# Masked attention: the first 512 columns of each unit but a job's last are turned by DMA and multiplied one unit later

## The chip, the cores and the metric

The kernel runs on one core of one Trainium2 chip. The metric is the device time of one execution in microseconds (us). The engines are named as in the profile: PE (TensorE, matmuls; PEld are its weight loads), DVE (VectorE), ACT (ScalarE), POOL (GpSimd) and SP (SyncE, which issues the DMA transfers here). Each engine executes its own instructions in order and waits on semaphores for the others.

## The reference, cut to what matters

Two layers over 1024 tokens of width 1024. Layer one holds a sparse attention ("A", in which a top-256 selection masks the keys) and a banded attention ("B"); layer two holds three kinds of one attention ("C") and a latent attention ("D"). The change touches A only:

```python
def dsa_attention(q, k, v, qi, ki, wi, k_sel):
    ...
        score = jnp.where(causal[None], score, -jnp.inf)
        _, idx = lax.top_k(score, k_sel)
        ...
        s = jnp.einsum('bqgrd,bqkgd->bqgrk', qb, ks) * scale
        p = masked_softmax(s, valid[:, :, None, None, :])
        o = jnp.einsum('bqgrk,bqkgd->bqgrd', p.astype(v.dtype), vs)
```

There are 8 blocks of 128 queries, and 8 heads that share keys and values in two groups of four. The kernel computes all causal scores and adds a mask of the selection, which gives the same softmax.

## The kernel before, in words

*Jobs and units.* `attn_gen` (L618) writes all four attentions as a list of jobs. A job of A (`job_a`, L1007) is one block i of 128 queries and one group g of four heads; its row of keys has nk = 128 (i + 1) columns. The list of A is g = 0, i = 0 to 7, then g = 1, i = 0 to 7 (L1183). A job is cut into units of `per` heads, four where nk is up to 256, two up to 512, one above. So i = 0, 1 have one unit, i = 2, 3 two, i = 4 to 7 four.

*One unit.* PE multiplies queries and keys into PSUM (L680, tile psS, up to 512 columns at a time). DVE adds the mask, takes the row extreme and writes the row to SBUF (L683, tile pt, three buffers). ACT prepares the bias (L687) and takes exp in place (L689). The values are then multiplied with the weights p, and for that p must lie with keys on the partitions: it has to be turned, and it is needed as a 16-bit high part and a 16-bit low part. A unit's columns are turned in groups of up to four tiles of 128 x 128, and each group goes one way:

- `p`: four PE transposes into PSUM (L730, psT), ACT copies the high part (L733, hp), DVE subtracts for the low part (L734);
- `q`: the same transposes, ACT copies the PSUM tile to SBUF (L737, sg), POOL makes the high part (L738) and the low part (L739). sg has the tag of hl, so both share its two buffers (HLB = 2);
- `d`, `g`, `l`: no PE transpose. ACT copies the high part straight from pt (L710, hl), DVE (`d`) or POOL (`g`, `l`) subtracts for the low part (L711), and one DMA transpose on SP's queue turns both into ht (L713, two buffers, HTB = 2).

After that PE multiplies three times per tile (L660, L661, L663). With `l` the multiplication is put on the list `late` (L715) and written behind the last group of the following unit (L744).

*Which way.* L705 gives `l` to the first group of a unit if the job says `late` and the unit isn't the job's last; otherwise the way is the next one of a cycle (`WAYS`): 'ppq' for A with g = 0, 'pq' with g = 1. Jobs of C (two of its three kinds) and D already say `late`, and their cycles hold 'p' alone. B has the cycle 'g'.

*Order.* Turning is written some groups behind the scores (`tlag`, L801), the values behind that. `L.run` (L1183) puts other work, the fill, beside attention at a ratio of the costs that the yields name: projections that are still missing, loading the output-projection weights, and `mix_ab` (rows of the finished attention are loaded, gated and turned by POOL and PE, and split by ACT and DVE). The output projection itself (`c_out`, L520 to L522, added to x at L1160) is written after the attention. This written order is a priority only: a planner orders each engine's instructions ahead of the run by its own cost estimates, takes an instruction when its inputs and a buffer are there, and so also moves later work, such as the output projection, into gaps. The reloads of x (L1201) use large buffers that masks, keys and other tiles hold until A's scores are done.

Of the kernel before, what the change touches and what calls it, by code (L numbers as in the profile page):

```python
# [184 lines left out]
def trunk(ctx: ExitStack, tc: tile.TileContext, A, out):  # L185
# [430 lines left out]
    ways = [cycle(w) for w in WAYS]  # L616
# [152 lines left out]
    def softmax_norm(mul=None):  # L769

        def norm(nm, sm, box, sink=None):
            yield
            if sink is not None:
                es = st.tile([P, 4], F32, name="es")
                V.tensor_tensor(es, nm, sink, OP.subtract)
                yield
                S.activation(es, es, AF.Exp)
                yield
                V.scalar_tensor_tensor(sm, sm, 1e-30, es, op0=OP.max, op1=OP.add)
            else:  # L780
                V.tensor_scalar(sm, sm, 1e-30, None, op0=OP.max)
            rs = st.tile([P, 4], F32, name="rs", bufs=6)
            V.reciprocal(rs, sm)
            if mul:
                mul(rs)
            box.append(rs)
        return norm

    def causal(nk):
        return lambda c, w: mk[:, 768 - w:] if c + w == nk else mk[:, P:P + w]  # L790

    def plain(m):
        return lambda c, w: m[:, c:c + w]

    def gqa(qs, j, kst, t0):
        def passes(h):
            q = qs[:, h % 2, j, h // 2]
            return [(q, lambda a, b: kst[:, 0, t0 + a:t0 + b]), (q, lambda a, b: kst[:, 1, t0 + a:t0 + b])]
        return passes
# [4 lines left out]
    def store_o(dst, i, c0, inv):  # L804
        def fin(po, f):
            m = wk.tile([P, 256], F32, name="mx", bufs=3)
            V.scalar_tensor_tensor(m.rearrange("p (h d) -> p h d", h=4), po, inv, bcast(f, 64), op0=OP.mult,
                                   op1=OP.mult)
            if dst is not None:
                nc.sync.dma_start(dst[i * P:(i + 1) * P, c0:c0 + 256], m)  # L810
            return m
        return fin
# [12 lines left out]
    def blk(t, i):  # L825

        return t[0] if i == 2 else t[1][:, OFF[i]:OFF[i] + (i + 1) * P]
# [179 lines left out]
    def job_a(i, g):  # L1007
        def start():
            nk = (i + 1) * P
            vh, vl = B["vha"], B["vla"]  # L1010
            f0 = store_o(od if g == 0 else None, i, 256 * g, B["vsca"][0][1])

            def fin(po, f):
                B["m", i] = f0(po, f)
                L.done.add(("oa", g, i))
            mask = causal(nk) if i < 2 else plain(blk(B["hi"], i).bitcast(BF16))
            return (gqa(B["qs", "a", g, i - i % 2], i % 2, B["ka"][g], 0), mask,
                    lambda kt, h: vh[:, kt, 64 * g:64 * g + 64], lambda kt, h: vl[:, kt, 64 * g:64 * g + 64],
                    lambda h: 3e38, fin)
        need = [("qa", g, i - i % 2), ("ka", i - i % 2), ("va", i)] + ([("mask", i)] if i >= 2 else [])  # L1020
        return dict(need=need, nk=(i + 1) * P, npass=2, start=start,
                    norm=softmax_norm(), tlag=tlag, way=ways[2 + g],
                    free=give_qs if i % 2 else None)

    XS = [slot("xs", F32)[:, 0:2048].rearrange("p (j n) -> p j n", j=2) for _ in range(NT // 2)]
# [155 lines left out]
    FM = fa_then()  # L1181
    L.run(attn_gen(jobs(job_b, 0, BO[0]) + jobs(job_b, 1, BO[1])), FA, BR, aux=tk, arate=TA)
    L.run(attn_gen(jobs(job_a, 0, AO[0]) + jobs(job_a, 1, AO[1])), FM, AR, aux=tk, arate=TA)  # L1183
    L.pump(FM)
    L.flush()
# [682 lines left out]
```

## Time and profile before

| | |
|---|---|
| median of 3 executions | 1532.42 us (1530.67 to 1533.38) |
| profiled execution | 1533.38 us |
| its span | 1531.6 us |
| PE busy in the span | 1334.1 us (87%) |
| PEld busy | 1218.5 us (80%) |
| DVE busy | 1106.3 us (72%) |
| ACT busy | 940.1 us (61%) |
| POOL busy | 820.4 us (54%) |

Busy time is the time in which an engine was executing an instruction; matmuls are pipelined, so overlapping matmuls count once and a busy PE need not be at its peak. In the timeline views a row begins with the start in us and the time taken in us; "xN" is a number of merged instructions, and a bracket at the end is the idle time before it with what ended it. In the views of one tile or line, three numbers with slashes are the shortest, median and longest duration in ns.

### The profile page before, as it was taken

The page shows a single profiled execution, that of the slowest core. Times are in us where ns is not written, and L with a number is a line of the kernel's source. Part 1 is how long each engine was busy: PE and PEld are TensorE (multiplying, and loading weights), DVE is VectorE, ACT ScalarE, POOL GpSimd, SP SyncE. Part 2 cuts the span into 40 slices and gives each one's busy share as a digit, 9 for nine tenths or more (in the row PEclk, how much of TensorE's full clock was granted, in tenths as well). Part 3 has the DMA queues.
Part 4 walks back from the last instruction along what each step waited for, and adds up shares of the span by engine and source line. Part 5 has one row for each costly group of instructions (what it writes and reads, how often), then busy time and mean ns, then how long its engine had stood idle before and what let it go on. Part 6 is the DMA issues. An engine that isn't in the chain of part 4 may idle for free. (4 is left out here: it accounts for less than half of the span.)

```text
span 1531.6 us, 34278 instructions
## 1 busy us (share of the span) xinstructions
PE 1334.1 (87%) x12132; PEld 1218.5 (80%) x12132; DVE 1106.3 (72%) x3409; ACT 940.1 (61%) x2683; POOL 820.4 (54%) x1058
## 2 busy tenths in 40 slices
PE   5998889888268899999999998999988668879998
PEld 5998788878157698999999986899967456768887
DVE  5387877888977865176367677876778989987652
ACT  5355578877668864164335667846677567856531
POOL 6899549897457584235355333352233465745440
PEclk9999999999569999999999999999998869999999
DMA  6311363322132333142212434212243323334442
GB/s 202 94 29 32 73 129 81 80 55 67 26 92 61 99 109 105 43 159 66 57 28 68 100 70 84 63 51 67 60 67 73 90 63 75 68 87 104 124 129 76
DMA packets 208939, 122.83 MB, mean 80 GB/s; under 512 B 141696, under 2 KB 193664, under 8 KB 208768
## 3 DMA queue, kind: packets, MB, share of 16 engines
q1 hardware_dynamic: 208768, 120.65, 31.5%
q8 instruction: 95, 1.56, 0.4%
q14 instruction: 76, 0.62, 0.1%
HBM read 67.65 MB, written 23.07 MB: 59 GB/s over the span
## 5 line engine op out<-in xcount | busy, mean ns | idle before, releaser
L520 PE MATMUL pp<-whi,Rh 128*128 128x256 f32 (+4 forms) x1648 | 481.1, 292 | 20.8 <-DVE zst L611 8.0
L522 PE MATMUL pp<-whi,Rl 128*128 128x256 f32 (+4 forms) x1648 | 476.9, 290 | 0.0
L521 PE MATMUL pp<-wlo,Rh 128*128 128x256 f32 (+4 forms) x1648 | 475.3, 289 | 0.7 <-POOL wlo L477 0.7
L520 PEld LDWEIGHTS pp<-whi,Rh 128*128 128x128 f32 x1648 | 317.2, 193 | 27.0 <-DVE zst L611 8.1
L521 PEld LDWEIGHTS pp<-wlo,Rh 128*128 128x128 f32 x1648 | 317.1, 192 | 2.3 <-POOL wlo L477 0.9
L522 PEld LDWEIGHTS pp<-whi,Rl 128*128 128x128 f32 x1648 | 316.9, 192 | 1.1
L689 ACT ACTIVATE pt<-pt,nm 128x256 f32<-128x256 f32 (+8 forms) x384 | 244.1, 638 | 5.4
L477 POOL TENSOR_TENSOR wlo<-wraw,whi 128x256 fp32r<-128x256 f32 (+4 forms) x208 | 162.7, 792 | 137.3 <-ACT whi L476 131.4
L711 POOL TENSOR_TENSOR hl<-pt,hl 128x512 f16<-128x512 f32 x114 | 137.1, 1205 | 148.5 <-ACT hl L710 121.5
L476 ACT ACTIVATE whi<-wraw 128x256 fp32r<-128x256 f32 (+4 forms) x208 | 83.2, 416 | 128.0 <-DMA wraw<-in_cd_w_in 42.1
L730 PE MATMUL psT<-identf,pt 128*128 128x128 f32 x800 | 145.1, 286 | 11.0 <-ACT pt L689 5.1
L733 ACT ACTIVATE hp<-psT 128x512 f16<-128x512 f32 (+3 forms) x241 | 108.2, 461 | 62.4 <-PE psT L730 57.5
L734 DVE TENSOR_TENSOR hp<-psT,hp 128x512 f16<-128x512 f32 (+3 forms) x241 | 123.3, 520 | 18.2 <-ACT hp L733 16.7
L683 DVE CUSTOM_DVE_ANT_0 pt<-psS,mk 128x512 f32<-128x512 f32 (+4 forms) x208 | 107.1, 521 | 40.5 <-PE psS L680 29.3
L730 PEld LDWEIGHTS psT<-identf,pt 128*128 128x128 f32 x800 | 95.3, 145 | 23.6 <-ACT pt L689 11.4
L687 ACT ACTIVATE nm<-nm 128x1 f32<-128x1 f32 (+2 forms) x208 | 41.6, 200 | 96.4 <-DVE nm L683 95.6
L663 PEld LDWEIGHTS <-hp 128*128 128x128 f16 x800 | 72.9, 99 | 29.2 <-DVE hp L734 17.6
L660 PEld LDWEIGHTS <-hp 128*128 128x128 f16 x800 | 74.4, 99 | 22.0 <-issue 7.5
L710 ACT ACTIVATE hl<-pt 128x512 f16<-128x512 f32 x114 | 70.9, 626 | 13.9 <-DMA ht<-hl 13.3
L661 PEld LDWEIGHTS <-hp 128*128 128x128 f16 x800 | 74.6, 99 | 2.8 <-issue 1.7
L689 ACT ACTIVATION_READ_ACCUMULATOR pt<-pt,nm 128x1 f32 x384 | 73.0, 190 | 0.0
L680 PE MATMUL psS<-kd,qhl 128*128 128x512 f32 (+4 forms) x192 | 57.4, 380 | 14.5 <-DVE nm L683 11.9
(326 smaller groups left out, 3764.0 us busy)
## 6 DMA issues: line engine op xcount, KB each, us to landing
wraw<-in_cd_w_in SPq DMA_DIRECT2D x72, 128.0 KB, 2.1
wraw<-in_ab_w_in SPq DMA_DIRECT2D x56, 128.0 KB, 2.5
xs<-in_x SPq DMA_DIRECT2D x8, 512.0 KB, 6.0
od<-mx SPq DMA_DIRECT2D x32, 128.0 KB, 1.9
wraw<-in_ab_w_out SPq DMA_DIRECT2D x32, 128.0 KB, 2.2
x<-in_x SPq DMA_DIRECT2D x8, 512.0 KB, 4.5
mo<-od SPq DMA_DIRECT2D x16, 256.0 KB, 2.9
nz<-zdr SPq DMA_DIRECT2D x16, 256.0 KB, 2.9
```

The costliest lines, as they stand in the source:

```text
L476: S.activation(hi[:, :o], raw[:, :o], AF.Copy)
L477: G.tensor_tensor(lo[:, :o], raw[:, :o], hi[:, :o].bitcast(F32), OP.subtract)
L520: T.matmul(ps, xh, hi[:, :n], start=q == 0 and k == 0, stop=False)
L521: T.matmul(ps, xh, lo[:, :n], start=False, stop=False)
L522: T.matmul(ps, xl, hi[:, :n], start=False, stop=q == 3 and k == 1)
L661: T.matmul(dst, ph[:, a], vl(kt, h), start=False, stop=False)
L683: V.tensor_tensor_reduce(pt[:, j * nk + c:j * nk + c + w], ps[:, at:at + w], mask(c, w), -1.0, first, op0=OP.add, op1=OP.min, accum_out=low)
L689: S.activation(pt[:, j * nk:(j + 1) * nk], pt[:, j * nk:(j + 1) * nk], AF.Exp, scale=-1.0, bias=nm[:, h:h + 1], accum_out=sm[:, h:h + 1])
L711: (V if way[-1] == "d" else G).tensor_tensor(hl[:, w:], pt[:, o:o + w], hl[:, :w], OP.subtract)
L730: T.transpose(pT[:, a], pt[:, o:o + P], identf)
L733: S.activation(ph, pT[:, :n], AF.Copy)
L734: V.tensor_tensor(pl, pT[:, :n], ph, OP.subtract)
```

## The change

A's jobs, too, say `late=True`. L705 then gives `l` to the first group (four tiles, 512 columns) of every unit of A but a job's last; the other groups go on drawing from their cycles.

```diff
@@ job_a
         return dict(need=need, nk=(i + 1) * P, npass=2, start=start,
-                    norm=softmax_norm(), tlag=tlag, way=ways[2 + g],
+                    norm=softmax_norm(), tlag=tlag, late=True, way=ways[2 + g],
                     free=give_qs if i % 2 else None)
```

## Rows read from the trace of the kernel before

**Rows 1.** Windows: stretch, length, busy PE, PEld, DVE, ACT, POOL (count), clock, DMA share, GB/s.
```profile
447.00:525.00 78.00, 69.88 (x815) 58.58 (x813) 64.81 (x191) 67.13 (x182) 45.66 (x59) 0.98 0.23 69
525.00:600.00 75.00, 67.95 (x821) 63.10 (x819) 46.94 (x134) 49.06 (x120) 56.26 (x69) 1.00 0.41 119
600.00:700.00 100.00, 99.07 (x820) 98.05 (x821) 48.12 (x134) 34.31 (x82) 28.43 (x40) 0.98 0.25 83
```

**Rows 2.** Timeline of DVE: the instruction that closes a job.
```profile
504.81 0.47 DVE L807 SCALAR_TENSOR_TENSOR mx<-po,vs_e,rs 128x256 f32<-128x256 f32 x1
...
516.46 0.48 DVE L807 SCALAR_TENSOR_TENSOR mx<-po,vs_e,rs 128x256 f32<-128x256 f32 x1
...
601.67 0.48 DVE L807 SCALAR_TENSOR_TENSOR mx<-po,vs_e,rs 128x256 f32<-128x256 f32 x1
```

**Rows 3.** Timeline of SP's queue, then of PE, at the second half's end.
```profile
587.84 1.97 SPq L1201 DMA_DIRECT2D x<-in_x  x4
...
600.57 0.58 PE L520 MATMUL pp<-whi,Rh 128*128 128x256 f32 x1 [1.98 <-DVE x L1160]
```

**Rows 4.** Timeline of PE around one group of transposes.
```profile
556.75 0.60 PE L730 MATMUL psT<-identf,pt 128*128 128x128 f32 x4
557.11 0.36 PE L522 MATMUL pp<-whi,Rl 128*128 128x256 f32 x1
557.31 0.28 PE L520 MATMUL pp<-whi,Rh 128*128 128x256 f32 x1
557.43 0.28 PE L521 MATMUL pp<-wlo,Rh 128*128 128x256 f32 x1
```

**Rows 5.** Tiles hp and sg, 447 to 600: the ways p and q.
```profile
L733 ACT ACTIVATE hp<-psT x51: 256/576/637, 447.3 to 595.1; 128x512 f16<-128x512 f32 x27, 128x256 f16<-128x256 f32 x10, 128x128 f16<-128x128 f32 x7, 128x384 f16<-128x384 f32 x7
...
L737 ACT ACTIVATE sg<-psT x35: 278/597/633, 454.2 to 593.9; 128x512 f32<-128x512 f32 x31, 128x256 f32<-128x256 f32 x2, 128x128 f32<-128x128 f32 x1, 128x384 f32<-128x384 f32 x1
L738 POOL TENSOR_SCALAR hp<-sg x35: 323/618/644, 454.9 to 594.6; 128x512 f16<-128x512 f32 x31, 128x256 f16<-128x256 f32 x2, 128x128 f16<-128x128 f32 x1, 128x384 f16<-128x384 f32 x1
L739 POOL TENSOR_TENSOR hp<-sg,hp x35: 426/1163/1174, 455.8 to 596.6; 128x512 f16<-128x512 f32 x31, 128x256 f16<-128x256 f32 x2, 128x128 f16<-128x128 f32 x1, 128x384 f16<-128x384 f32 x1
```

**Rows 6.** Tiles hl and ht, 850 to 1220 (attention C); last, who waited for ht: us, times.
```profile
L710 ACT ACTIVATE hl<-pt x56: 614/626/668, 854.7 to 1191.7; 128x512 f16<-128x512 f32 x56
L711 POOL TENSOR_TENSOR hl<-pt,hl x56: 1152/1164/1279, 855.4 to 1192.4; 128x512 f16<-128x512 f32 x56
L713 SPq DMA_TRANSPOSE ht<-hl x56: 1231/1232/2197, 856.6 to 1194.8; - x56
...
  PE po L660: 8.5, 10
  ACT hl L710: 5.9, 10
...
DMA to landing us min/median/max: 3.0/3.1/4.8
```

**Rows 7.** Waits of ACT (total, times, longest): 447 to 525, then 525 to 600.
```profile
ACT hp L733 <- PE psT L730: 2.4, 5, 0.8
...
ACT sg L737 <- PE psT L730: 1.1, 2, 0.7
...
ACT hp L733 <- PE psT L730: 7.9, 6, 2.7
```

**Rows 8.** Windows, columns as in rows 1.
```profile
460.00:480.00 20.00, 15.93 (x191) 12.77 (x189) 13.64 (x42) 17.05 (x46) 19.59 (x28) 1.00 0.30 90
```

**Rows 9.** Waits of PE and of POOL, 525 to 600.
```profile
PE po L660 <- POOL hp L738: 2.7, 1, 2.7
PE po L663 <- POOL hp L739: 1.4, 1, 1.4
...
POOL mo L1112 <- DMA mo<-od: 1.7, 2, 1.3
```

**Rows 10.** Windows for line 520 alone: stretch, length, busy PE, PEld, clock, DMA share, GB/s.
```profile
470.00:498.00 28.00, 0.00 (x0) 0.00 (x0) 0.94 0.14 41
```

## The prediction

> **What bounds the kernel now.** I first read busy time by stretch over the whole span, to find the masked attention and what follows it. It runs from 447 to about 600 us as two halves, one per group of heads, and the table splits them [rows 1]. In the first half ScalarE (ACT) is busy 67.1 of 78 us, TensorE (PE) 69.9, VectorE (DVE) 64.8: three engines in step, none with much room. In the second half ACT falls to 49.1 of 75 while PE stays at 68.0; from 600 to 700 PE is busy 99.1 of 100. The second half is longer because output-projection matmuls, which need finished rows of both groups, come in between: PE carries both.
>
> Then the ends of jobs, by the VectorE instruction that closes each [rows 2]: the last job of the first half takes 516.46 - 504.81 = 11.65 us, 2.9 per unit (one head of 1024 keys); the second half closes 601.67 - 516.46 = 85.2 us after the first.
>
> What hands the end on is a load. The last four reloads of x go out at 587.84, when the last scores have released their buffers, and PE waits 1.98 us for them before the out-projection goes on at 600.57 [rows 3]. From there PE is full, so if the last scores come earlier by d, the kernel ends earlier by about d.
>
> **The change part by part.** Jobs i = 2, 3 have two units and i = 4 to 7 have four; all but a job's last give their first 512 columns to the new way: 2 + 12 = 14 groups per half, 28 in all, of four 128x128 tiles each. Groups no longer drawn from the cycles 'ppq' and 'pq' shift all later draws. Walking the cycles through the 86 groups gives: p 51 becomes 35, q 35 becomes 23. Of these, p of four tiles 27 to 21, q of four tiles 31 to 9, q of fewer 4 to 14.
>
> *Removed from PE.* 112 transposes. Four start at 556.75, the next matmul at 557.11; the one after comes 0.20 later where the usual step is 0.12 [rows 4]. So a group costs 0.36 + 0.08 = 0.44 us, and 14 per half cost 6.2 us. In the second half I count it in full: -6.2. In the first I count nothing, because PE's waits there are on the other engines and ACT sets the pace; the ends are 0 and -6.2, and the row nearest is ACT's 67.1 of 78. The Trainium skill (Perfetto Trace Analysis, section Identifying the Most-Contended Engine) holds that matmul busy time misleads, as matmuls are pipelined, and that weight-load busy time is to be read for TensorE. By the matmul column both halves are about 90% PE, and the term would be -12.4; by the weight loads (58.6 of 78, then 63.1 of 75, [rows 1]) PE is the fullest engine in the second half only, and it is -6.2.
>
> *ACT.* A copy pt to hl of 0.626 us [rows 6] for a copy psT to sg of 0.597 or to hp of 0.576 [rows 5]: with 0.59 for the old one, 14 x 0.036 = +0.5 us in the first half. ACT also waited there 2.4 + 1.1 = 3.5 us for transposes [rows 7]; half the four-tile groups go, so I take -1.75 (ends 0, -3.5). New: the copy needs one of two hl buffers, which the q way's sg shares. In the later attention, which turns its 56 groups this way already, ACT waited 5.9 us for a transfer to free one [rows 6], 0.105 per holder; 14 + 9 holders give +2.4. Lower end 0, upper end 23 x 0.59 = +13.6, each holder stalling as long as one of those ten waits did; I take the mean, the nearest row. First half: +0.5 - 1.75 + 2.4 = +1.1. In the second half ACT has 26 idle us: 0.
>
> *VectorE.* Sixteen p subtractions fewer, on an engine with 13 idle us in the first half and 28 in the second [rows 1]: 0, and no more than the 3.5 us that ACT's term allows, since ACT comes next in step.
>
> *GpSimd (POOL).* 22 four-tile q groups less, at 0.618 + 1.163 = 1.78 us: -39.2. Ten smaller ones more, between 0.75 and 1.78: about +11. 28 subtractions of 1.164: +32.6. Net +4, but unevenly: first half 10 q of four down to 4 (-10.7), one small more (+1), 14 late (+16.3), +6.8 in all. POOL is full from 460 to 480, 19.6 of 20 us [rows 8]. Two or three late groups fall there; they are not needed for a unit, which covers their 1.16 us, so 0 (upper end +3.5). In the second half PE waited 2.7 + 1.4 = 4.1 us for POOL's halves of q groups [rows 9], in the stretch where POOL is also preparing constants. Four-tile q drop from 21 to 5 but small ones appear: I take half, -2.0 (ends 0, -4.1).
>
> *The transfers and the late multiplication.* 28 DMA transposes, 3.1 us to landing [rows 6], used one unit (2.9 us or more) later. After ACT's 0.63 and POOL's 1.16, landing is 4.9 us from the copy's start, so the margin is thin and may be exceeded. The later attention shows the price: PE waited 8.5 us for 56 such groups, 0.15 each; 14 in the second half: +2.1 (ends 0, and 0.85 for every group, +11.9). In the first half the wait lies beside ACT's work.
>
> *SyncE's queue.* 28 x 1.232 = 34.5 us of issue in 153 us, each also held until POOL has written hl. Behind it wait the stores of od, the loads of mo, nz, zx and the weights. POOL waited only 1.7 us for mo in the second half [rows 9], so loads come ahead of use: 0; if each of the 16 loads of mo were 1.23 us late, +19.7 at most.
>
> *Fill pace.* A late group has no transpose step in the written order, so 28 x 440 ns less fill is asked for. The fill has nothing left to give from 470 to 498 us, zero projection matmuls [rows 10]: 0.
>
> Sum: -6.2 - 2.0 + 2.1 + 1.1 = -5.0 us. The profiled execution took 1533.38 us (span 1531.6 and 1.8 around it); -5.0 makes 1528.4. It lies 0.96 above the median of three, 1532.42, so on that scale: 1527.4 us.
>
> **The rivals.**
>
> *A. Both halves give.* The first half also turns out to be paced by PE and transposes, and transfers hide: -6.2 - 4.1 - 3.5 + 0.5 = -13.3, 1519.1. For it: ACT's 10.9 idle us in the first half. Against: its busy share.
>
> *B. No change.* The planner fills the freed PE time with out-projection matmuls sooner, attention keeps its pace, and the last scores stay at 587; PE then waits longer for x. Only the first half's +1.1 is left: 1533.5. For it: the 1.98 us wait shows that this work runs out before x lands. Against: in the second half ACT waited 7.9 us for transposes on the crowded PE [rows 7], so attention does wait for PE.
>
> *C. Slower: the two hl buffers.* A late group holds one for 4.9 us, a q group for 0.60 + 0.62 + 1.16 = 2.4. A unit with one late group and 9/20 of a q holds 4.9 + 1.1 = 6.0, on two buffers 3.0 us per unit, against today's 2.9. ACT works in order, so its next exp waits too. With that term at its upper end the first half loses 0.5 - 1.75 + 13.6 = 12.4, the second half's -6.1 kept: +6.3, 1538.7. It decides once ACT's waits for ht<-hl in the first half pass 6.1 + 1.25 = 7.4 us. For it: the later attentions, where such stalls were small, turn their other groups by p alone, so nothing shares the buffers there. Against: the planner knows the buffers and can put other ACT work first.
>
> *D. Slower: values too late.* If all 28 waited 0.85 us on PE, +23.8 - 8.2 + 1.1 = +16.7: 1549.1. The Trainium skill (VectorE: DVE Perf Modes, section Rules for kernel authors) advises transposing 128x128 on TensorE where PSUM will do, and the crossbar DMA otherwise; by it this edit takes the dearer path. In the trace the transfer is the longer (3.1 us against 0.44), which is a price only where it is waited for: ten matmuls waited, on 56 groups [rows 6].
>
> **How the numbers follow.** Likeliest case 0.45, A 0.12, B 0.20, C 0.18, D 0.05. About 0.2% (3.1 us) is what a measurement here can tell from no change. The likeliest case spreads from 1523 to 1530, nearly all of it beyond 3.1 us: with A, 0.53 faster. B and the edge of the likeliest case: 0.20 same. C, D and B's tail: 0.27 slower. Range: 1518 reaches A; 1540 reaches C; D and the ends beyond lie outside. Likeliest case alone: 1523 to 1530. A stretch of low granted clock (0.94 from 470 to 498, [rows 10]) may come or go with PE's load; it is inside the range.
>
> **What would show it.** Right: last scores and last x reloads near 582 instead of 587.8, PE's busy time lower by about 12 us before 600, the first half's end (516.5) moved by less than 2 us, waits of PE for ht<-hl in the masked stretch of 2 to 6 us. A would show the first half's end near 510. B: reloads of x still at 587 and a longer PE wait for x. C: ACT waiting 7.4 us or more for ht<-hl, and the first half ending after 520. D: PE waits for ht<-hl above 15 us. I am wrong altogether if the stretch after 600 takes back what was won, or if the planner orders other stages differently and the difference lies outside 447 to 610.

## The result, and the profile after

The kernel after took 1570.39 us (median of 4 runs, 1562.49 to 1573.92), the one before, on the same chip, 1532.86 (1530.67 to 1533.38): a ratio of 1.0239, 95% interval 1.0209 to 1.0269. I had forecast 1527.4 and a range of 1518 to 1540. It is slower by 37.5 us, in the direction of rival C and far beyond its price.

Windows of the kernel after, columns as in [rows 1]: the three stretches of that group, the whole masked stretch, the stretch of [rows 8], and two short ones inside the first half.

```profile
447.00:525.00 78.00, 59.93 (x548) 44.59 (x546) 48.67 (x136) 53.43 (x141) 45.80 (x56) 0.83 0.39 90
525.00:600.00 75.00, 63.14 (x655) 49.22 (x654) 48.01 (x144) 50.75 (x135) 43.84 (x58) 0.94 0.50 117
600.00:700.00 100.00, 92.11 (x878) 89.88 (x874) 33.68 (x95) 27.43 (x61) 33.75 (x42) 0.97 0.40 111
...
447.00:626.00 179.00, 141.28 (x1451) 110.35 (x1450) 109.22 (x306) 114.14 (x298) 102.07 (x128) 0.88 0.51 119
...
460.00:480.00 20.00, 14.21 (x132) 11.24 (x130) 13.50 (x35) 14.91 (x41) 18.42 (x25) 0.80 0.38 102
...
475.00:489.00 14.00, 8.04 (x59) 5.93 (x59) 6.33 (x17) 6.58 (x19) 11.27 (x17) 0.50 0.45 110
496.00:503.00 7.00, 5.47 (x61) 3.65 (x61) 4.54 (x13) 5.16 (x12) 3.18 (x4) 1.00 0.39 55
```

Against [rows 1], every engine is busy for less of the first stretch: ACT 53.4 of 78 us instead of 67.1, PE 59.9 instead of 69.9. Nothing new is full. The engines wait for one another.

The VectorE instructions that close the last job of the first half and of the second, and the last x reloads on SP's queue, answering [rows 2] and [rows 3]:

```profile
535.52 0.48 DVE L807 SCALAR_TENSOR_TENSOR mx<-po,vs_e,rs 128x256 f32<-128x256 f32 x1
...
625.70 0.48 DVE L807 SCALAR_TENSOR_TENSOR mx<-po,vs_e,rs 128x256 f32<-128x256 f32 x1 [0.68 <-PE po L663]
```

```profile
609.84 0.87 SPq L1201 DMA_DIRECT2D x<-in_x  x2
```

The first half ends 19.1 us late (516.46 before), the second half takes 5.0 us longer (90.2 against 85.2), so attention A ends 24.0 us late. The last output-projection add (L1160) starts at 711.2 instead of 679.0, that is 32.2 late. Attention C, in the next layer, ends 31.1 late and the kernel 37.5. About two thirds of the loss arise in A, 8 us between A's end and the end of the output projection, 6 us in the last stage.

Waits in the kernel after, 447 to 626 (us in total, times, longest): first ACT, then SP's queue, then PE. [Rows 7] and [rows 9] are the views before.

```profile
ACT sg L737 <- DMA ht<-hl: 23.5, 13, 6.0
ACT nm L687 <- DVE nm L683: 12.4, 10, 2.5
...
ACT hl L710 <- DMA ht<-hl: 7.0, 7, 2.5
...
ACT hp L733 <- PE psT L730: 1.0, 1, 1.0
```

```profile
SPq L713 <- PE po L663: 30.9, 12, 7.5
```

```profile
PE psT L730 <- ACT sg L737: 14.1, 9, 5.2
...
PE po L663 <- POOL hp L739: 1.8, 5, 0.8
PE po L660 <- POOL hp L738: 1.2, 3, 0.9
...
PE po L660 <- DMA ht<-hl: 0.7, 1, 0.7
```

ACT waits 30.5 us for a transfer to free an hl buffer, and 23.5 of these stand ahead of the *q* copy, which has nothing to do with the transfer but draws from the same two buffers. SP waits 30.9 us for PE to free ht. The multiplication that uses the turned values waits for them only once, 0.7 us. So each link waits for the next in a circle, which one place shows. ACT's copies, SP's queue (the transposes, and weight loads between two of them) and PE, kernel after, with other rows between left out:

```profile
469.66 0.63 ACT L710 ACTIVATE hl<-pt 128x512 f16<-128x512 f32 x1
477.49 0.57 ACT L737 ACTIVATE sg<-psT 128x512 f32<-128x512 f32 x1
482.86 0.63 ACT L710 ACTIVATE hl<-pt 128x512 f16<-128x512 f32 x1
487.92 0.28 ACT L737 ACTIVATE sg<-psT 128x128 f32<-128x128 f32 x1 [4.43 <-DMA ht<-hl]
```

```profile
464.35 1.74 SPq L713 DMA_TRANSPOSE ht<-hl  x1
472.99 1.23 SPq L713 DMA_TRANSPOSE ht<-hl  x1
475.31 8.57 SPq L472 DMA_DIRECT2D wraw<-in_ab_w_out  x4
484.35 1.75 SPq L713 DMA_TRANSPOSE ht<-hl  x1
```

```profile
484.07 0.24 PE L663 MATMUL po<-vha,ht 128*128 128x64 f16 x1
...
488.25 0.69 PE L730 MATMUL psT<-identf,pt 128*128 128x128 f32 x2 [2.24 <-ACT sg L737]
```

The hl copy of 469.66 is the fourth in A, and the transpose of 484.35 the fourth. It is issued 14.7 us after the copy. The last thing to come free for it was ht: one late group, whose transpose was issued at 464.35, is multiplied only up to 484.07 (until 484.31). Its values are written behind the next unit's remaining group, and that group was a *q* whose copy, at 477.49, came right behind the landing (477.39) that freed an hl buffer. When the transfer lands, near 487.9, a copy of 0.28 us has held ACT for 4.43 us, and PE for 2.24 after it. The hl buffer was held for about 18 us.

The circle is not all that holds this group. SP's queue stood from 474.3 to 483.9 on four weight loads (L472), most of the time waiting for POOL, so the transpose could not have been issued before 483.9 in any case; and POOL, 18.4 of 20 us busy from 460 to 480, needed from 478.55 to 482.8 for the two parts of that *q* group. One place shows the order of the waits, then, and not their price; for that the experiments are needed. Over all 28 late groups, paired in order, the transpose is issued 5.15 us after its copy on average, and hl is held 8.8; in attention C before, over 56 groups, the transpose came after 2.2.

The tiles of the two ways over the same stretch, answering [rows 5] and [rows 6]:

```profile
L737 ACT ACTIVATE sg<-psT x23: 257/492/624, 455.6 to 619.6; 128x512 f32<-128x512 f32 x9, 128x256 f32<-128x256 f32 x5, 128x384 f32<-128x384 f32 x5, 128x128 f32<-128x128 f32 x4
```

```profile
L710 ACT ACTIVATE hl<-pt x28: 614/632/655, 455.1 to 610.4; 128x512 f16<-128x512 f32 x28
L711 POOL TENSOR_TENSOR hl<-pt,hl x28: 1151/1160/1182, 455.9 to 611.6; 128x512 f16<-128x512 f32 x28
L713 SPq DMA_TRANSPOSE ht<-hl x28: 1231/1232/2437, 457.1 to 621.2; - x28
...
DMA to landing us min/median/max: 3.0/3.5/5.5
```

Counts and durations are those of the prediction: 28 late groups, q 23 with 9 of four tiles, the copy 0.632 us, the subtraction 1.16. No instruction grew dear; the holding of buffers did.

### The profile page after: what moved, and what is told of

The parts are those of the page before. It is cut to its first block, busy times and chain, and to the rows that moved or that the text cites. A ratio compares the mean times of both kernels' runs of the same rounds, so it can differ in the third digit from the quotient of the medians.

```text
span 1569.1 us, 34146 instructions
## 1 busy us (share of the span) xinstructions
PE 1354.1 (86%) x12020; PEld 1223.1 (78%) x12020; DVE 1113.3 (71%) x3393; ACT 943.5 (60%) x2683; POOL 823.2 (52%) x1062
## 4 chain that ended last, share of the span: by engine, by line
PE 35%; DVE 16%; DMA 4%; ACT 3%; issue 3%; POOL 2%; POOLq 0%; ACTq 0%; SPq 0%; DVEq 0%
PE pp L520 6%; PE pp L522 6%; PE pp L521 5%; PE psS L680 4%; DMA ht<-hl 3%; DVE pt L683 3%; PE psT L730 2%; PE pp L1751 2%; PE pp L1753 2%; PE pp L1752 2%; DVE hp L734 1%; ACT pt L689 1%; PE po L660 1%; PE po L663 1%; DMA wraw<-in_cd_w_in 1%
## 5 line engine op out<-in xcount | busy, mean ns | idle before, releaser
L520 PE MATMUL pp<-whi,Rh 128*128 128x256 f32 (+4 forms) x1648 | 481.6, 293 | 19.1 <-DVE zst L611 7.6
L521 PE MATMUL pp<-wlo,Rh 128*128 128x256 f32 (+4 forms) x1648 | 476.3, 289 | 1.1 <-POOL wlo L477 1.1
L522 PE MATMUL pp<-whi,Rl 128*128 128x256 f32 (+4 forms) x1648 | 477.2, 290 | 0.0
L520 PEld LDWEIGHTS pp<-whi,Rh 128*128 128x128 f32 x1648 | 317.7, 193 | 25.4 <-DVE zst L611 7.8
L521 PEld LDWEIGHTS pp<-wlo,Rh 128*128 128x128 f32 x1648 | 317.5, 193 | 3.1 <-POOL wlo L477 1.6
L522 PEld LDWEIGHTS pp<-whi,Rl 128*128 128x128 f32 x1648 | 317.4, 193 | 1.0
L711 POOL TENSOR_TENSOR hl<-pt,hl 128x512 f16<-128x512 f32 x142 | 169.4, 1196 | 180.1 <-ACT hl L710 139.8
L730 PE MATMUL psT<-identf,pt 128*128 128x128 f32 x688 | 131.6, 293 | 25.1 <-ACT sg L737 14.1
L734 DVE TENSOR_TENSOR hp<-psT,hp 128x512 f16<-128x512 f32 (+3 forms) x225 | 115.2, 521 | 34.8 <-ACT hp L733 33.6
L683 DVE CUSTOM_DVE_ANT_0 pt<-psS,mk 128x512 f32<-128x512 f32 (+4 forms) x208 | 107.3, 522 | 39.5 <-PE psS L680 25.6
L733 ACT ACTIVATE hp<-psT 128x512 f16<-128x512 f32 (+3 forms) x225 | 101.0, 462 | 51.2 <-PE psT L730 48.4
L730 PEld LDWEIGHTS psT<-identf,pt 128*128 128x128 f32 x688 | 83.5, 147 | 40.0 <-ACT sg L737 17.1
L710 ACT ACTIVATE hl<-pt 128x512 f16<-128x512 f32 x142 | 88.6, 628 | 18.3 <-DMA ht<-hl 14.0
L663 PEld LDWEIGHTS <-hp 128*128 128x128 f16 x688 | 65.4, 102 | 26.0 <-DVE hp L734 14.5
L660 PEld LDWEIGHTS <-hp 128*128 128x128 f16 x688 | 66.6, 102 | 19.4 <-issue 6.9
L680 PE MATMUL psS<-ka,qs 128*128 128x512 f32 (+4 forms) x192 | 61.3, 418 | 17.9 <-DVE nm L683 15.2
L660 PEld LDWEIGHTS <-ht 128*128 128x128 f16 x568 | 54.8, 104 | 22.7 <-DMA ht<-hl 21.6
```

The lines of the kernel that those rows point to most:

```text
L520: T.matmul(ps, xh, hi[:, :n], start=q == 0 and k == 0, stop=False)
L521: T.matmul(ps, xh, lo[:, :n], start=False, stop=False)
L522: T.matmul(ps, xl, hi[:, :n], start=False, stop=q == 3 and k == 1)
L660: T.matmul(dst, ph[:, a], vh(kt, h), start=heads[0] == 0, stop=False)
L680: T.matmul(ps[:, at + a - c:at + b - c], lhs, rhs(a, b), start=n == 0, stop=n == len(pl_) - 1)
L683: V.tensor_tensor_reduce(pt[:, j * nk + c:j * nk + c + w], ps[:, at:at + w], mask(c, w), -1.0, first, op0=OP.add, op1=OP.min, accum_out=low)
```

## The experiments

My theory L: the loss is the circle just described, a shortage of hl buffers because sg draws from them too. Its rivals go by letters in the expectations, which say there what each holds. The table has each run's median, its ratio to the kernel before on the same chip (timed anew beside each group of runs), and from its trace when A's last job closes (L807), when the last output-projection add starts (L1160), and ACT's waits for ht<-hl from 447 to 626 (sg + hl). The times are medians, but the last three columns are read from one execution each, which can lie some us from the median: 1535.05 for p_before, 1539.20 for p_after, 1536.47 for own_sg, 1550.50 for own_sg_before.

| run | us | ratio [95%] | A | L1160 | waits |
|---|---|---|---|---|---|
| before | 1532.86 | 1 | 601.7 | 679.0 | none |
| after | 1570.39 | 1.0239 [1.0209, 1.0269] | 625.7 | 711.2 | 23.5 + 7.0 |
| sg_nz | 1569.93 | 1.0258 [1.0238, 1.0278] | 626.1 | 709.5 | 0 + 10.7 |
| htb3 | 1559.21 | 1.0171 [1.0143, 1.0200] | 610.8 | 696.9 | 14.3 + 2.7 |
| tlag1 | 1552.91 | 1.0139 [1.0112, 1.0167] | 617.9 | 700.5 | 13.1 + 4.1 |
| q_rest_p | 1551.28 | 1.0141 [1.0119, 1.0162] | 613.0 | 696.9 | 5.6 + 6.2 |
| own_sg | 1539.80 | 1.0073 [1.0044, 1.0102] | 601.1 | 683.6 | 0 + 7.6 |
| hpb3_after | 1572.94 | 1.0266 [1.0242, 1.0290] | 629.6 | 715.6 | 21.9 + 9.2 |
| hlb3 | 1541.38 | 1.0064 [1.0043, 1.0084] | 609.4 | 691.8 | 12.8 + 2.8 |
| sg_hp | 1540.04 | 1.0066 [1.0045, 1.0086] | 603.4 | 684.7 | 0 + 5.9 |
| hpb3_before | 1536.37 | 1.0031 [1.0013, 1.0049] | 608.3 | 685.9 | none |
| own_sg_before | 1548.69 | 1.0093 [1.0059, 1.0127] | 618.7 | 697.2 | none |
| p_before | 1538.66 | 1.0063 [1.0040, 1.0085] | 605.6 | 681.5 | none |
| p_after | 1535.57 | 1.0026 [1.0012, 1.0041] | 599.5 | 682.3 | 0 + 4.7 |
| p_tlag1 | 1538.66 | 1.0057 [1.0040, 1.0074] | 596.5 | 684.9 | 0 + 4.4 |
| late_g0 | 1557.05 | 1.0175 [1.0149, 1.0200] | 614.8 | 694.7 | 8.8 + 0.8 |
| late_g1 | 1562.25 | 1.0199 [1.0166, 1.0231] | 618.9 | 699.9 | 12.9 + 3.6 |
| own_sg_g1 | 1543.94 | 1.0086 [1.0066, 1.0107] | 599.6 | 688.4 | 0 + 6.7 |
| hlb3_hpb4 | 1540.13 | 1.0047 [1.0030, 1.0064] | 606.4 | 688.7 | 8.6 + 7.5 |
| own_sg_hpb4 | 1535.69 | 1.0038 [1.0020, 1.0056] | 599.7 | 682.0 | 0 + 7.5 |

### Is it the shared buffer?

*own_sg*: the change, with sg in one buffer of its own; hp pays with its fourth. *hpb3_after*: the change, with three hp buffers alone. *hlb3*: three hl buffers, still shared. *sg_hp*: sg from hp's four.

```diff
own_sg, own_sg_before:
-  sg = wk.tile([P, 4, P], F32, name="sg", tag="hl", bufs=HLB)
+  sg = wk.tile([P, 4, P], F32, name="sg", bufs=1)       # and HPB = 3
sg_hp:
+  sg = wk.tile([P, 4, P], F32, name="sg", tag="hp", bufs=HPB)
hlb3:         HLB = 3, HPB = 3
hpb3_after, hpb3_before:   HPB = 3
```

> The changed kernel with one buffer for sg alone (hp has three instead of four to make room), so sg and the late groups no longer share hl, and no other tile's ring is touched. In sg_nz the projection of the second half's queries moved into the stretch, since it uses nz too, so that run did not settle it. Theory L (a loop of waits: hl is freed by the transfer, the transfer needs ht, ht is freed by values that are written behind the next unit's rest group, and that group, where it is q, needs an hl buffer for sg): the link is cut, ACT's wait of sg for ht<-hl is gone, SyncE's wait for the values (30.9 us) falls under 12 us, time 1533 to 1548. Rival R (the link is POOL's order: q halves stand behind late subtractions, whatever buffer they use): SyncE's wait stays above 20 us, time 1555 or above.

> The changed kernel with 3 instead of 4 buffers for hp: the control for the runs with sg's own buffer, three ht buffers and three hl buffers. Theory L (sg and late groups sharing two hl buffers is the loss): at least the changed kernel's time, 1575 us (1566 to 1585). Rival H (the fourth hp buffer lets ScalarE run ahead into the shared buffers, so taking it away is what helped): 1538 to 1550.

> The changed kernel with three hl buffers, still shared by late groups and sg, and 3 for hp. Theory L as a shortage of holders: most of the loss gone, as with sg's own buffer, 1542 us (1535 to 1550). Rival S (the order, a q group that stands behind a late group in the same ring, costs whatever their number): above 1555.

> The changed kernel with sg drawn from the four hp buffers, so the hl buffers belong to late groups alone. Theory L: the ACT waits of sg for ht<-hl are gone, but a q group then holds two of four hp buffers; 1541 us (1534 to 1552). Rival M (late turning itself): 1550 or more.

With three hp buffers throughout, 1572.94 falls to 1539.80 when sg leaves hl, and to 1541.38 when hl has three buffers; with sg on hp's four it is 1540.04. Three ways of ending the shortage: by the ratios, which set the chips equal, they are worth 30, 31 and (against the change with its four hp) 26 us, and the hp count by itself did not help. Rivals H (of hpb3_after), S, M and R are refuted; only SP's wait for PE in own_sg, 14.7 us, stayed above the 12 that I had set for L. ACT's waits before and after, both with three hp buffers: the change (hpb3_after), then own_sg.

```profile
ACT sg L737 <- DMA ht<-hl: 21.9, 10, 6.8
...
ACT hl L710 <- DMA ht<-hl: 9.2, 6, 4.3
ACT hl L710 <- POOL hp L739: 5.5, 6, 1.7
```

```profile
ACT hl L710 <- DMA ht<-hl: 7.6, 9, 1.5
ACT sg L737 <- POOL hp L739: 5.8, 4, 3.8
```

The third buffer in hlb3 leaves 12.8 us of the sg wait, though, and A ends at 609.4 instead of 601.1. The q copy still stands behind late groups there, but three holders are enough for the time.

*sg_nz* moved sg to the ring of nz.

```diff
+  sg = wk.tile([P, 512], F32, name="sg", tag="nz", bufs=NZ).rearrange("p (a n) -> p a n", a=4)
```

> The changed kernel, but sg (the copy that the q way's POOL reads) takes its buffers from the four of tag nz instead of sharing the two of hl with the late groups; nothing else. Theory H (the shared ring: ACT's copy into sg waits for a late group's transfer to free an hl buffer, 23.5 us in the changed kernel's masked attention): that wait falls to under 3 us and the time from 1570 to 1530 to 1545. Rival T (the transfers themselves are held up because ht's two buffers are freed by values that come several units late; SyncE waited 30.9 us for them): the time stays at 1555 or above, and the copies into hl wait instead.

ACT's wait of sg for the transfer went (23.5 to 0), but the time did not move. By its number rival T was right, and L's range was missed; but the run changed two things. The planner ran 103 L520 matmuls fewer ahead of 447 us and 111 more in the masked stretch (165 instead of 54 there), and nz is the ring of the loads that mix the finished rows (POOL waited 15.8 us for them). So it is no clean test of L.

### The other links of the circle

```diff
htb3:      HTB = 3, HPB = 3
tlag1, p_tlag1:    norm=softmax_norm(), tlag=lambda n: 1, late=True, way=ways[2 + g],
q_rest_p:  way.append(("l" if c == 0 else "p") if jb.get("late") and h0 + per < 4 else next(jb["way"]))
```

> The changed kernel with three ht buffers instead of two; hp has three instead of four to make room. Theory H (hl shared with sg): sg still waits behind late groups, time 1555 or above. Rival T (ht is freed too late): SyncE's wait of 30.9 us for the values falls under 10 us, hl is freed sooner, and the time is 1535 to 1550.

> The changed kernel, but A's jobs let one group lag behind the scores instead of two where a unit has two groups. With late groups a unit hands only one group to that list, so two groups are two units of lag, and ht is held about four units in the written order. Theory H: the ring is as shared as before, 1555 or above. Rival T: the values free ht a unit sooner, SyncE's wait for them falls under 15 us, 1530 to 1550.

> The changed kernel, but the rest group of a unit with a late group always goes p; the cycles serve only the other groups (i = 0, 1 and each job's last unit), which may still be q and share hl. Theory L: the loop is open in every late unit, time 1526 to 1540, ACT's wait of sg for ht<-hl under 5 us. Rival R: the same, since few q are left; a third view, that late turning costs by the transfers alone, expects 1550 or above.

A third ht buffer halves SP's wait for PE (30.9 to 14.6) and by the ratios takes 10 us off (15 against hpb3_after, which has its three hp buffers); writing the values one group closer takes 15 us off, and so does a *p* for the rest group of a late unit. Each weakens the circle, none breaks it. htb3's time was H's; tlag1, at 1552.9 with SP's wait at 24.7, missed both theories. For q_rest_p I had expected 1526 to 1540: a miss. Its trace still has 12 *q* groups (11 of four tiles), among them those of a job's last unit, which is turned right behind a late group, and ACT still waits 11.8 us for ht<-hl and 6.3 for POOL to release sg. That these last units carry the rest of the loss is argued from the cycle, not tested.

### The other way: no q at all

*p_before* and *p_after* are the two kernels with A's cycles set to 'p' (L74), so that nothing shares hl; *p_tlag1* adds the shorter lag.

```diff
-WAYS = ('g', 'g', 'ppq', 'pq', 'p', 'p', 'p', 'p')
+WAYS = ('g', 'g', 'p', 'p', 'p', 'p', 'p', 'p')
```

> The changed kernel with the way cycles of A set to p alone, so no q group and no sg exists in A (DVE makes the low part of 58 groups instead of POOL's 23). Theory H: no sharing is left, no wait of ACT for a transfer above 5 us, time 1525 to 1545. Rival T: ht is still freed late, 1550 or above.

> The kernel before with A's cycles set to p alone and no late groups: the control for p_after (1535.6 us). If late turning itself pays once no q is there, this is slower than p_after by 3 us or more, 1539 to 1548: PE has 112 transposes more, DVE and ACT the same order of work. If it does not pay, 1528 to 1535.

> p_after with one group of lag in A instead of two. Theory L has nothing left to free here: within 4 us of p_after, 1532 to 1540. If lateness in units still holds the transfers up (SyncE waited 6.1 us for values in p_after), 1528 to 1533.

Here late turning does not lose: 1535.57 against 1538.66 (timed in two groups of runs; the intervals of the ratios touch at 1.0040). p_before lies just below the 1539 that I had set for "it pays", and p_tlag1, as L said, within 4 us of p_after by the medians. In the profiled executions A ends 6.1 us earlier in p_after, close to the sum I had forecast, though its execution was the longer one. But the last output-projection add starts 0.8 us later.

### Halves, and what the buffers cost

*late_g0* and *late_g1* give `late` to one half only, *own_sg_g1* to the second half with sg apart; *hpb3_before* and *own_sg_before* are the kernel before with those buffers.

```diff
late_g0:   late=g == 0,
late_g1, own_sg_g1:   late=g == 1,
```

> The change in the first half of the masked attention's units only (14 late groups), the second half as before. Theory L (the q way's sg takes the hl buffers that late groups hold; the loss arises where it is exposed): the changed kernel's trace places +23 us of its +24 in the first half, so this keeps most of the loss: 1553 us (1545 to 1562). Rival O (turning the values a unit late costs by itself, the same for each of the 28 late groups): half of the +37 us, 1549 (1544 to 1553), and the same as the kernel with the second half alone.

> The change in the second half of the units only (14 late groups). Theory L: the second half itself ended 1 us late in the changed kernel, but it did some 9 us less of TensorE's work, of which the out-projection's adds later showed 8; so 1540 us (1533 to 1547). Rival O: as the first half alone, 1549 (1544 to 1553). The prediction's own sum for this half (-6.2 +2.1) would give 1526.

> Second half late only, and sg in a buffer of its own (paid by 3 instead of 4 buffers for hp). Theory L: the shared buffer was this half's cost, so its gain (-4) shows apart from what the fourth hp buffer was worth: 1531 us (1526 to 1537), at least 4 below the second half alone with sg shared. Rival O: no different from the second half alone.

> The kernel before with 3 instead of 4 buffers for hp, the control for the run with sg's own buffer (1539.8, +9.4 over before). Theory L with nothing else: within 3 us of before (1530 to 1534), and the +9.4 is what is left of late turning itself. Rival B3: the missing hp buffer is that +9.4, so 1536 to 1541 here too.

> The kernel before with sg in a buffer of its own and 3 for hp: what late turning costs when nothing is shared is own_sg's 1539.8 less this. Theory L with the prediction's gain: this is 1542 us (1538 to 1547), so that late turning gains a little. Rival M (late turning itself costs the +9): 1530 to 1536.

The "+23 in the first half" in the first of these is 19.1, as shown above. late_g0, at 1557, lies in L's range and above O's, but L's range rests on that wrong number. late_g1 at 1562 missed both theories: the first half closes at 515.0, so the second took 103.9 instead of 85.2, with 16.5 us of ACT's waits. The second half of the changed kernel lost only 5.0 us, but it also carried less output-projection work: 38 matmuls of L520 between the two ends, where late_g1 had 50 and the kernel before 60. One half is enough to set off the circle, and the two do not add up. With sg apart the same half costs 18 us less (1543.94), L's direction, but 7 us above the range I gave.

The fourth hp buffer is worth about 4 us (hpb3_before, on the side of B3), so it is part of own_sg's +9. sg in a single buffer and three for hp cost 14 without late groups, by the ratio (own_sg_before; A ends at 618.7), more than expected; *q* groups then follow each other through one buffer, and ACT waits 7.3 us for POOL to free it, against 1.5 before. With these buffers late turning ends A 17.6 us earlier and the last add 13.6 earlier, but these two executions lie at opposite ends of their runs, and the two ratios overlap.

### Is the predicted gain there when nothing is short?

Both runs keep four hp buffers, and pay with one of 14 pairs of the projections' weight buffers (WBF = 13): *hlb3_hpb4* has HLB = 3, *own_sg_hpb4* the sg of own_sg.

> The changed kernel with three shared hl buffers and all four for hp; the room comes from the projections' weight buffers (13 pairs instead of 14). Theory L: about 4 us below the run with three hl and three hp buffers, 1537 us (1531 to 1543). Rival P (the prediction's gain is real where nothing is short): 1526 (1522 to 1530). Rival M (late turning costs by itself): 1541 or more.

> The changed kernel with sg in one buffer of its own and all four for hp, paid the same way. Theory L: 1536 us (1530 to 1542). Rival P: 1526 (1522 to 1530). Rival M: 1541 or more.

1540.13 and 1535.69: no gain over before, 0.38% slower [0.20, 0.56] at best. Rival P, my own sum, had 1522 to 1530 and is missed by both; M's 1541 is not reached either, and L's ranges hold. But neither run is one in which nothing is short: 16.1 and 7.5 us of ACT's waits for transfers are left, a single sg buffer has a cost of its own (own_sg_before), and the kernel before with 13 weight pairs was not run. Whether the gain would show without these stays open; the one pair that shares nothing, p_before and p_after, shows 3.1 us, with intervals that touch. In own_sg_hpb4 A ends at 599.7 (601.7 before) and its last x reload starts at 587.3 (589.4), but the output projection ends 3.0 us later. Windows of the kernel before, then of own_sg_hpb4, over the stretch of A before:

```profile
447.00:602.00 155.00, 139.26 (x1639) 123.12 (x1637) 113.75 (x328) 116.19 (x302) 101.93 (x128) 0.98 0.32 93
```

```profile
447.00:602.00 155.00, 130.18 (x1488) 110.95 (x1488) 105.97 (x304) 112.13 (x295) 103.96 (x130) 0.93 0.60 138
```

PE is busy for 9.1 us less while A ends 2.0 us earlier: most of the freed time is idle time, and the clock is a little lower. Part of it is work put off: the second half holds 49 L520 matmuls instead of 60 (50 against 62 in p_after and p_before). Behind A eight of them, with their L521 and L522, go by every 2.85 us, so 11 are about 4 us by estimate, most of the 4.9 us by which the way from A's end to the last add grew. In this execution the later stages win the 3.0 us back (1533.15 us, the kernel before 1533.38), so the trace does not show where the 0.38% of the median lie.

And the rows that the output projection needs come later. The transposes that turn the gated rows (L1119, written by `mix_ab`), first and last start, before and in own_sg_hpb4:

```profile
L1119 PE MATMUL psT<-identf,mo x48: 270/273/307, 522.6 to 589.2; 128*128 128x128 f32 x48
```

```profile
L1119 PE MATMUL psT<-identf,mo x48: 271/273/456, 534.6 to 602.8; 128*128 128x128 f32 x48
```

Before, the last of them start 12.5 us ahead of A's last job; here 3.1 us behind it. p_before and p_after show the same (594.3 and 602.4), and the kernel after has 631.5. Two causes can do that. `mix_ab` advances in the written order by one step for each step that attention yields, and a late group yields none. Or its loads stand on SP's queue behind transposes that wait: SP held L713 for PE's L663 6.4 us between 540 and 605. The trace divides them in part. The first of these transposes is already 12.0 us late, nearly as much as the last (13.6). Its multiplication on POOL (L1112) starts 7.1 us later (506.3 instead of 499.2), when its load lands; from there to the transpose it takes 28.3 us instead of 23.4, with nothing left to load. So the queue is not the whole of it; for the rest no run tells the two apart. Of the versions tried none beats the kernel before.

## Why the prediction was wrong, by its own steps

*ACT's term, and rival C: the step that failed.* For the first half I took the price of a holder from attention C, 0.105 us each, and got +2.4, with 13.6 as the upper end; for the second half I put 0, because ACT had 26 idle us. Measured: ACT waited 11.6 us for ht<-hl in the first half and 19.0 in the second. The first half lost 19.1 us where I had +1.1, the second 5.0 where I had -6.1, and 13.5 more came behind A, where I had nothing. The marks I had named for C, 7.4 us and an end after 520, were both passed (11.6, and 535.5), and the mechanism was C's. I gave it 0.18.

C's price of the wait, 13.6, was near; its 1538.7 was not. One reason is the holding time. 4.9 us belongs to a transpose issued as soon as hl is written. Here hl was held 8.8 us on average, and even where nothing shares it, in p_after, 7.1: there SP waited before L713 11.9 us for POOL's L711 and 6.1 for PE. By C's own formula 8.8 makes (8.8 + 1.1) / 2 = 4.95 us per unit against 2.9, +29 for the 14 late units of the first half, where 4.9 had given 0.1 per unit. That is an estimate after the fact, and no test: the 8.8 has the stalls in it, covers both halves, and gives more than the 19.1 seen. Another is that a stalled ACT delays the other engines: in the first half ACT's own waits for DVE's L683 rose from 2.1 to 7.1 us and the granted clock fell from 0.98 to 0.82. How the 19.1 us divide among these was not separated. The third is the second half's gain of 6.1, which C kept, as if the idle time there would cover the waits; late_g1 lost 18.7 us in that half alone.

*PE: -6.2.* The transposes went (176 records of L730 in A instead of 286), and PE's busy time before 600 fell by more than 12 us, but as waiting. Where the circle is broken, A ends 2.0 (own_sg_hpb4, against before) or 6.1 us (p_after, against p_before) earlier. So the term may be real in A, but some 4 us of either are output-projection work put off, by the estimate above.

*The hand-over: wrong as well.* "If the last scores come earlier by d, the kernel ends earlier by about d" failed in all four runs in which the last x reload goes out earlier than before (own_sg, sg_hp, p_after, own_sg_hpb4): their last add starts 3.0 to 5.7 us later. From A's end to the last L1160 it is 77.4 us before, 82.3 in own_sg_hpb4, 82.8 in p_after, 75.9 in p_before. The reading under it was wrong too. The 1.98 us that PE waits in [rows 3] are not a wait for x. DVE, kernel before, with other rows between left out:

```profile
593.04 0.42 DVE L1160 TENSOR_TENSOR x<-pp,x 128x256 f32<-128x256 f32 x1 [0.52 <-DMA x<-in_x]
...
598.96 1.22 DVE L595 TENSOR_REDUCE vs_m<-pt 128x1 f32<-128x1024 f32 x1 [2.55 <-DMA pt<-in_cd_w_in]
600.10 0.41 DVE L1160 TENSOR_TENSOR x<-pp,x 128x256 f32<-128x256 f32 x1
```

The last x landed at 597.13. The add of 600.10, for which PE waited, stood on DVE behind L595, which waited 2.55 us for a weight of the next layer. I also took PE's busy 99 of 100 us after 600 as proof that the earlier start is all it lacks. The output projection also depends on `mix_ab`, whose pace I priced at nothing twice: under "Fill pace", from a stretch around 480 us where it is not yet running, and under SP's queue.

*VectorE, POOL: nothing, and -2.0.* Small as forecast: PE's waits for POOL's halves from 525 to 600 went from 4.1 to 2.9 us. (POOL's first half adds up to +6.6, not +6.8; nothing rests on it.) *The late multiplication: +2.1.* PE waited 0.7 us for ht<-hl. Rival D's mechanism, values too late on PE, does not occur; it was the writer of hl that paid. *SyncE: 0.* Wrong in the changed kernel: SP held L713 30.9 us for PE.

*Rivals A and B.* A's early first half does not occur in any run with q; in p_after the first half ends at 516.1, where p_before has 514.7. own_sg_hpb4 ends near the 1533.5 that B gave, but that is luck: B had the projection moving forward into the freed PE time and then waiting for x, and here the projection moved back and x came earlier.

The Trainium skill (VectorE: DVE Perf Modes, section Rules for kernel authors) prefers TensorE for a 128x128 transpose where PSUM will do. The result goes its way, and p_after shows that it need not: with *p* alone, late turning cost nothing against the same kernel without it.

## What to carry to other kernels

A buffer's holding time is not a property of the operation alone: here it ran on until the consumer's place in the order came up and the queue was free (8.8 us, where 4.9 had been reckoned). When a change brings a second kind of user to a small ring, follow one buffer round the whole circle (copy, transfer, consumer, what stands ahead of the consumer) before borrowing a stall from a stage where the ring has one user. And when an engine is relieved, name the work that will take its time and check that its inputs come earlier too; otherwise the time turns into idle time.

## What the hardware showed that I had not expected

The granted clock fell along with the waits of another engine. In the kernel after it was 0.50 (the lower level, 1.2 GHz) from 475 to 489, after PE had been busy for 4.45 of the 7 us before, at a clock of 0.79; it was 1.00 (2.4 GHz) again from 496 to 503. Over 447 to 626 it is 0.88, and 0.98 before. So a stall on ACT is paid again: between 483 and 486 a multiplication of ht took 0.24 us, the median over A is 0.193. How much of the 24 us by which A ended late is the clock was not separated.
